# The first token tile leads the projection at a layer's beginning

## The chip, the cores and the metric

The kernel runs on one core of one Trainium2 chip. The metric is the time of one execution on the device in microseconds (us), the median of several runs. The engines are named as in the profile: PE is TensorE (products), PEld its weight loads, DVE VectorE, ACT ScalarE, POOL GpSimd, SP the queue that issues DMAs.

## The reference

Two layers of a decoder, in float32, for 256 tokens of 2048 features. Each layer is a norm, a mixer with an input and an output projection, a second norm and a residual:

```python
def rms_norm(x, g):
    xf = x.astype(jnp.float32)
    y = xf * lax.rsqrt(jnp.mean(xf * xf, axis=-1, keepdims=True) + RMS_EPS)
    return (y * g.astype(jnp.float32)).astype(x.dtype)
...
for layer in range(DEPTH):            # 2
    g_pre, g_post, p = layer_params[layer]
    h = rms_norm(x, g_pre)
    h = even_mixer(h, *p) if layer % 2 == 0 else odd_mixer(h, *p)
    x = x + rms_norm(h, g_post)
...
# even_mixer (RG-LRU and mLSTM):  u = h @ w_in (2048 x 8192); ...; y @ w_out (4096 x 2048)
# odd_mixer (RWKV-7):             u = h @ w_in (2048 x 16384); loras of h; ...; y @ w_out (4096 x 2048)
```

## The kernel before

**Tokens and features.** The 256 tokens are two token tiles of 128, counted by `tt`. Norms have tokens on the partitions; `x` lies in four tiles `xs[c]` of [128, 2 token tiles, 512 features]. The input projections have features on the partitions, so the normed tokens are turned by products: `to_features` multiplies a 128x128 block of `xs` with `dg[tt]`, a diagonal matrix of the token tile's 1/rms (`scale`, made from `rstd`), and so turns and scales in one. Each such f32 product shows as two records in the trace (`mb<-dg,xq` and `gb<-dg,xq` in layer 0, `xr` in layer 1).

**Two parts.** Projections run in fp32r. For precision each operand is split into a high part and the rest: `hh`, `hl` for the tokens (ACT copies with the norm's weight as scale, DVE subtracts), `whi`, `wlo` for the weights (`split_w`, the same two engines). Each product of a block is then three: hh with whi, hl with whi, hh with wlo.

**The input projection.** `in_proj` makes 512 output features at a time, in two PSUM banks `gb`; its depth of 2048 is cut into 8 pieces of two k-tiles. A piece is one DMA of 512 KB (`raw`, 4 buffers), one split (`whi`, `wlo`, 3 buffers each), and 24 products (`in_mms`: 8 blocks x 3) of 128x128 weights with 256 columns, both token tiles at once. Piece `pc` reads k-tiles 2 pc and 2 pc + 1 of `h`, that is half of one of the four tiles `hh[c]`, `hl[c]`. Layer 0 has 16 such projections of 512 features, layer 1 has 32 and the loras.

**The output projection.** `out_proj` has tokens on the partitions, four chunks of 512 features. In the last chunk the last pieces (`NLAST` = 3 and up to `ROOM` = 3 more) go token tile by token tile, so that `evac` (sum of squares, `rstd`, product with the post-norm's weight) and `after` (residual `xs`, its squares, the next norm's `scale`) of tile 0 run beside the products of tile 1. What `evac` and `after` emit for tile 1 comes behind the last product.

**The beginning of a layer.** In layer 0: load `x` tile by tile, keep-warm products (`W0` = 14, bf16, read by nothing), squares of both tiles on ACT, both `scale`, then `to_features`. In layer 1: `to_features` directly behind `out_proj` of layer 0, with `W1` = 6 and `W2` = 10 keep-warm products before and between the first transposes. `to_features` turns tile 0 of c = 0, 1 and 2, then for each c turns tile 1 (for c = 3 both) and splits 256 columns at a time into `hh` and `hl`: 16 ACT and 16 DVE operations a layer. Then `in_proj` begins:

```python
banks = [gbank(), gbank()]
for pc in range(8):
    in_mms(banks, *split_w(load_w(wsrc[pc])), pc, h, 4, 0.44)
return banks
```

**Order.** PE issues in the order of the program (`InOrder`). ACT, DVE, POOL and SP are ordered when the program is built, by priorities: weight splits are raised by `AHEAD` = 1000 and the last tile's `evac` and `after` by 2000, and with `Behind` what is emitted after a weight split on ACT or DVE stays behind it. Steps of the mixers are woven between the products of a projection by amounts of product work (`tick`). All engines work in order once built.

**Lines.** The helpers record their operations under one line: products are L116, transposes by identity L119, ACT and DVE operations L132, DMAs of weight pieces L217; the two POOL steps of `rstd` are L312 (scale by 1/D and add EPS) and L314 (power -0.5), the residual's store is L720.

## Time and profile before

| | |
|---|---|
| three runs | 1916.69, 1919.91, 1921.01 us (median 1919.91) |
| profiled execution | span 1912.7 us from its first to its last instruction; the profile gives no other time of it |
| busy | PE 98%, weight loads 91%, DVE 73%, ACT 55%, POOL 3% |
| mean granted clock | 0.997 |
| products | 16498 records, each with a weight load |

The runs are times of whole executions, the span is that of one other, profiled execution of the same kernel; the median is 7.2 us above it. In the timeline a row has start, length, engine, line, operation, `out<-in`, shapes, count and, in brackets, the engine's idle time before it and what ended that. In the groups, `| busy us, mean ns of one | idle before`. The granted clock (PEclk) is 1.00 at full speed.

### The profile page before, as it was taken

The page shows a single profiled execution, that of the slowest core. Times are in us where ns is not written, and L with a number is a line of the kernel's source. Part 1 is how long each engine was busy: PE and PEld are TensorE (multiplying, and loading weights), DVE is VectorE, ACT ScalarE, POOL GpSimd, SP SyncE. Part 2 cuts the span into 40 slices and gives each one's busy share as a digit, 9 for nine tenths or more (in the row PEclk, how much of TensorE's full clock was granted, in tenths as well). Part 3 has the DMA queues.
Part 4 walks back from the last instruction along what each step waited for, and adds up shares of the span by engine and source line. Part 5 has one row for each costly group of instructions (what it writes and reads, how often), then busy time and mean ns, then how long its engine had stood idle before and what let it go on. Part 6 is the DMA issues. An engine that isn't in the chain of part 4 may idle for free.

```text
span 1912.7 us, 39517 instructions
## 1 busy us (share of the span) xinstructions
PE 1883.4 (98%) x16498; PEld 1747.9 (91%) x16498; DVE 1395.3 (73%) x2302; ACT 1044.1 (55%) x1609; POOL 60.4 (3%) x84
## 2 busy tenths in 40 slices
PE   8999999999999999999999999999999999999998
PEld 7999999999888899989999999999999999997886
DVE  5667777757554569969689689597796896895544
ACT  5444666645444546555565555655655655555442
POOL 0000000000000100000000000000000000000000
PEclk9999999999999999999999999999999999999999
DMA  7433545455666444434444434344344443356664
GB/s 250 142 133 111 177 162 169 155 171 194 215 208 195 168 147 135 152 118 144 133 136 138 133 130 155 111 147 149 113 150 139 136 136 131 122 187 203 211 202 156
DMA packets 86947, 299.63 MB, mean 157 GB/s; under 512 B 9576, under 2 KB 12392, under 8 KB 86768
## 3 DMA queue, kind: packets, MB, share of 16 engines
q1 hardware_dynamic: 86768, 297.11, 47.2%
q8 instruction: 129, 2.11, 0.5%
q14 instruction: 50, 0.41, 0.1%
HBM read 289.20 MB, written 7.86 MB: 155 GB/s over the span
## 4 chain that ended last, share of the span: by engine, by line
PE 93%; DVE 4%; ACT 1%; issue 1%; DMA 0%; POOL 0%; SPq 0%; DVEq 0%; POOLq 0%; ACTq 0%
PE gb L116 75%; PE mb L116 17%; DVE wlo L132 2%; PE mb L119 1%; DVE wb L132 1%; ACT whi L132 1%; DMA xq<-in_x_dram 0%; DVE rt L132 0%; DVE Tb L132 0%; DVE tf L132 0%; DVE Ab L132 0%; DVE yT L132 0%; ACT ZT L132 0%; ACT vt L132 0%; DVE At L132 0%
## 5 line engine op out<-in xcount | busy, mean ns | idle before, releaser
L132 DVE TENSOR_TENSOR wlo<-raw,whi 128x1024 fp32r<-128x1024 f32 x509 | 619.9, 1219 | 338.0 <-ACT whi L132 304.5
L132 ACT CAST whi<-raw 128x1024 fp32r<-128x1024 f32 x509 | 532.6, 1048 | 557.3 <-PE gb L116 512.3
L116 PE MATMUL gb<-hh,whi 128*128 128x256 f32 x3120 | 790.5, 289 | 2.8 <-ACT whi L132 2.8
L116 PE MATMUL gb<-hl,whi 128*128 128x256 f32 x3120 | 770.6, 283 | 0.0
L116 PEld LDWEIGHTS gb<-hh,whi 128*128 128x128 f32 x3120 | 596.7, 191 | 13.6 <-ACT whi L132 3.7
L116 PEld LDWEIGHTS gb<-hl,whi 128*128 128x128 f32 x3120 | 597.5, 192 | 0.8
L116 PE MATMUL gb<-hh,wlo 128*128 128x256 f32 x3120 | 453.5, 286 | 0.0
L116 PEld LDWEIGHTS gb<-hh,wlo 128*128 128x128 f32 x3120 | 404.9, 191 | 4.2 <-issue 0.7
L116 PE MATMUL gb<-whi,yl 128*128 128x512 f32 x500 | 136.9, 392 | 0.5 <-DVE yl L132 0.5
L116 PE MATMUL gb<-whi,yh 128*128 128x512 f32 x500 | 136.5, 392 | 0.0
L116 PE MATMUL gb<-wlo,yh 128*128 128x512 f32 x500 | 135.7, 390 | 0.0
L116 PEld LDWEIGHTS gb<-whi,yl 128*128 128x128 f32 x500 | 93.2, 188 | 20.4 <-DVE yl L132 0.9
L116 PEld LDWEIGHTS gb<-wlo,yh 128*128 128x128 f32 x500 | 93.5, 188 | 19.8
L116 PEld LDWEIGHTS gb<-whi,yh 128*128 128x128 f32 x500 | 93.0, 188 | 19.3
L132 DVE TENSOR_TENSOR Tb<-Tb,tf 64x31 f32<-64x31 f32 (+15 forms) x248 | 82.6, 333 | 6.1
L132 DVE TENSOR_TENSOR tf<-Ab,Tb 64x31 f32<-64x31 f32 (+15 forms) x248 | 81.9, 330 | 4.5
L116 PE MATMUL mb<-AR,BK 64*128 64x128 f32 (+1 forms) x1024 | 58.0, 253 | 7.0 <-DVE AR L132 6.0
L116 PEld LDWEIGHTS mb<-AR,BK 64*128 64x128 f32 (+1 forms) x1024 | 50.2, 161 | 13.3 <-PE gb L116 7.1
L132 DVE TENSOR_TENSOR UV<-mb,Gn 64x256 f32<-64x256 f32 x64 | 26.9, 421 | 34.5 <-PE mb L116 33.4
L132 ACT ACTIVATE zz<-kP,dv 128x256 f32<-128x256 f32 x64 | 32.3, 505 | 22.9 <-DVE kP L132 12.4
L116 PEld LDWEIGHTS mb<-UV,At 128*64 128x64 f32 (+1 forms) x1024 | 35.0, 137 | 10.3 <-issue 2.5
L1125 POOL TENSOR_TENSOR vr<-vr,mhalf 128x8 f32<-128x8 f32 x16 | 28.3, 1771 | 499.4 <-DVE vr L132 499.4
(258 smaller groups left out, 1855.9 us busy)
## 6 DMA issues: line engine op xcount, KB each, us to landing
raw<-in_w_in_dram SPq DMA_DIRECT2D x384, 512.0 KB, 3.3
raw<-in_w_out_dram SPq DMA_DIRECT2D x128, 512.0 KB, 4.3
y1d<-zt SPq DMA_DIRECT2D x7, 512.0 KB, 3.9
yraw<-y1d SPq DMA_DIRECT2D x7, 512.0 KB, 4.3
l<-in_lora_dram SPq DMA_DIRECT2D x8, 384.0 KB, 4.6
xq<-in_x_dram SPq DMA_DIRECT2D x8, 256.0 KB, 5.2
lw<-in_lruw_dram SPq DMA_DIRECT2D x4, 512.0 KB, 4.6
xr<-in_x_dram SPq DMA_DIRECT2D x8, 256.0 KB, 6.0
```

Of the source, the lines that this page charges most:

```text
L116: return self._chain(self.eng.matmul(*a, **k))
L119: return self._chain(self.eng.transpose(**k))
L132: r = op(*a, **k)
L1125: pool.tensor_tensor(vr, vr, mhalf[:, 0:8], ALU.pow)
```

## The change

1. `to_features` works by token tile. `turn(tt)` makes all 16 transposes of one tile, one `mb` bank for each c, and returns four splits; each is 4 ACT and 4 DVE operations of 128 columns. It returns `h` and the turn of tile 0, and leaves the turn of tile 1 in the list `rest`. Its keep-warm products (`W1`, `W2`) are gone; `W0` is 20.
2. The first `in_proj` of a layer finds `rest` filled. It loads and splits `LEAD` = 3 pieces, makes their 72 products with the 128 columns of tile 0, then the transposes and splits of tile 1, then the same 72 products with tile 1; pieces 3 to 7 go as before.
3. In layer 0 tile 0 is scaled, turned and split before the squares of tile 1 are emitted. In layer 1 `out_proj` gets `between`: behind the last products of tile 1 come the transposes of the next layer's tile 0; the first of their splits goes between `evac` and `after`, the others behind `after`.
4. `rstd` loses its POOL step L312: the squares are scaled by D ** -0.5 on ACT (`RD`), and EPS is a fifth column of the sums, set once by a POOL memset.

Comments are dropped as well. The diff without these, cut to its core:

```diff
-W0, W1, W2 = 14, 6, 10
+W0 = 20
+LEAD = 3
...
-    def in_mms(banks, hi, lo, pc, h, nft, tick):
+    def in_mms(banks, hi, lo, pc, h, nft, tick, tts=None):
+        to = 0 if tts is None else tts * P
+        tn = T if tts is None else P
         def mm(part, kk, f, hx, first=False, last=False):
-            pe.matmul(banks[f // 2][:, (f % 2) * T:(f % 2 + 1) * T], lhsT=part[:, kk, f * P:(f + 1) * P], rhs=hx,
-                      start=first, stop=last, skip_group_check=True)
+            pe.matmul(banks[f // 2][:, (f % 2) * T + to:(f % 2) * T + to + tn], lhsT=part[:, kk, f * P:(f + 1) * P],
+                      rhs=hx[:, to:to + tn], start=first, stop=last, skip_group_check=True)
...
+    rest = []
     def in_proj(wsrc, h):
         banks = [gbank(), gbank()]
-        for pc in range(8):
+        lead = LEAD if rest else 0
+        ws = [split_w(load_w(wsrc[pc])) for pc in range(lead)]
+        for tt in range(2):
+            for pc in range(lead):
+                in_mms(banks, *ws[pc], pc, h, 4, 0.22, tt)
+            if rest:
+                for split in rest.pop()():
+                    split()
+        for pc in range(lead, 8):
             in_mms(banks, *split_w(load_w(wsrc[pc])), pc, h, 4, 0.44)
...
     # out_proj, last pieces of the last chunk, for each tt
+                parts = between() if tt and between else []
                 with tc.high_priority(offset=2 * AHEAD):
                     evac(c, banks, (tt,))
+                    for split in parts[0:1]:
+                        split()
                     after(tt)
+                for split in parts[1:]:
+                    split()
...
     def rstd(ss):
         dve.tensor_reduce(ms, ss, mybir.AxisListType.X, ADD)
-        pool.tensor_scalar(ms, ms, 1.0 / D, EPS, MUL, ADD)
         pool.tensor_tensor(rs, ms, mhalf[:, 0:1], ALU.pow)
     def sums(n):
-        return [sp.tile([P, 4], F32, name=f"{n}{tt}", tag=f"{n}{tt}") for tt in range(2)]
+        ts = [sp.tile([P, 5], F32, name=f"{n}{tt}", tag=f"{n}{tt}") for tt in range(2)]
+        for t in ts:
+            pool.memset(t[:, 4:5], EPS)
+        return ts
...
-    def to_features(xs, dg, g, warm):
+    def to_features(xs, dg, g):
-        h = []
-        banks[2] = [gbank(), gbank()]
-        keep_warm(warm[0], banks[2][0])
-        for c in range(2):
-            turn(c, 0)
-        keep_warm(warm[1], banks[2][0])
-        turn(2, 0)
-        for c in range(4):
-            if c == 3:
-                turn(c, 0)
-            turn(c, 1)
-            ... (hh, hl of 256 columns, i = 0 to 3)
+        h = [tuple(hp.tile([P, 4, T], F32R, name=n, tag="hp") for n in ("hh", "hl")) for c in range(4)]
+        def turn(tt):
+            ts, parts = slice(tt * P, (tt + 1) * P), []
+            def split(c, b):
+                hh, hl = h[c]
+                for f in range(4):
+                    bf = b[:, f * P:(f + 1) * P]
+                    activ(hh[:, f, ts], bf, AF.Copy, scale=g(4 * c + f))
+                    dve.scalar_tensor_tensor(hl[:, f, ts], bf, g(4 * c + f), hh[:, f, ts].bitcast(F32), MUL, SUB)
+            for c in range(4):
+                b = mbank()
+                for f in range(4):
+                    pe.matmul(b[:, f * P:(f + 1) * P], lhsT=xs[c][:, tt, f * P:(f + 1) * P], rhs=dg[tt],
+                              start=(f == 0), stop=True, skip_group_check=True)
+                parts.append(lambda c=c, b=b: split(c, b))
+            return parts
+        rest.extend([lambda: [], lambda: turn(1)])
+        return h, lambda: turn(0)
...
     # layer 0
         for tt in range(2):
             for c in range(4):
-                activ(sq[c][:, tt, :], xs[c][:, tt, :], AF.Square, acc=ss[tt][:, c:c + 1])
-        h = to_features(xs, [scale(ss[tt], s0) for tt in range(2)], lambda i: vs0("pre", i), (0, 0))
+                activ(sq[c][:, tt, :], xs[c][:, tt, :], AF.Square, scale=RD, acc=ss[tt][:, c:c + 1])
+            dg.append(scale(ss[tt], s0))
+            if tt == 0:
+                for split in first():
+                    split()
```

## The prediction

> **What bounds the kernel now.** I read the page first: the busy shares (part 1) and the chain that ended last (part 4).

> ```profile
> span 1912.7 us, 39517 instructions
> ...
> PE 1883.4 (98%) x16498; PEld 1747.9 (91%) x16498; DVE 1395.3 (73%) x2302; ACT 1044.1 (55%) x1609; POOL 60.4 (3%) x84
> ...
> PE 93%; DVE 4%; ACT 1%; issue 1%; DMA 0%; POOL 0%; SPq 0%; DVEq 0%; POOLq 0%; ACTq 0%
> ```

> TensorE is busy in 98% of the span and carries 93% of the chain. A product added to TensorE therefore costs its full cadence, unless it falls into one of the few holes. The change works in two holes, at the beginning of each layer, so I read next the timeline of TensorE there. Columns: start, length, engine, line, what it does, count, and in brackets the idle time before it. First layer 0, with the cast and the rest of the first weight piece from ScalarE and VectorE:

> ```profile
> 9.64 2.05 PE L116 MATMUL mb<-dg,xq 128*128 128x128 f32 x16 [3.60 <-DVE dg L132]
> 11.53 1.06 PE L116 MATMUL gb<-dg,xq 128*128 128x128 f32 x8
> 12.72 1.05 ACT L132 CAST whi<-raw 128x1024 fp32r<-128x1024 f32 x1 [0.94 <-DMA raw<-in_w_in_dram]
> 13.26 2.05 PE L116 MATMUL mb<-dg,xq 128*128 128x128 f32 x16 [0.68 <-DVE dg L132]
> 13.80 1.23 DVE L132 TENSOR_TENSOR wlo<-raw,whi 128x1024 fp32r<-128x1024 f32 x1 [0.59 <-ACT whi L132]
> 15.15 1.06 PE L116 MATMUL gb<-dg,xq 128*128 128x128 f32 x8
> 16.81 2.02 PE L116 MATMUL mb<-dg,xq 128*128 128x128 f32 x16 [0.60 <-PE gb L116]
> 18.59 0.36 PE L116 MATMUL gb<-hh,whi 128*128 128x256 f32 x1
> ...
> 27.29 0.28 PE L116 MATMUL gb<-hh,whi 128*128 128x256 f32 x1
> ```

> From 9.64 to 18.59 there are 64 transpose records (two per f32 product, 32 per token tile) and less than 2 us of idle time; at 18.59 the projection begins, and at 27.29 its fourth piece. Then layer 1, the same view, with what VectorE does ahead of the first piece's low part:

> ```profile
> 642.71 0.61 PE L116 MATMUL gb<-wlo,yh 128*128 128x512 f32 x2
> 643.17 1.47 PE L116 MATMUL gb<-ones 128*128 128x512 bf16 x6
> 644.22 0.68 DVE L132 TENSOR_TENSOR og<-gb,gp 128x512 f32<-128x512 f32 x1
> 644.48 1.95 PE L116 MATMUL mb<-dg,xr 128*128 128x128 f32 x16
> 645.25 2.74 DVE L132 SCALAR_TENSOR_TENSOR xr<-og,rs,xr 128x512 f32<-128x512 f32 x4 [0.35 <-POOL rs L314]
> 646.26 2.32 PE L116 MATMUL gb<-ones 128*128 128x512 bf16 x10
> 647.91 1.22 DVE L132 TENSOR_TENSOR wlo<-raw,whi 128x1024 fp32r<-128x1024 f32 x1
> 648.42 1.05 PE L116 MATMUL gb<-dg,xr 128*128 128x128 f32 x8
> 651.38 2.47 PE L116 MATMUL mb<-dg,xr 128*128 128x128 f32 x16 [1.91 <-DVE dg L132]
> 653.64 1.92 PE L116 MATMUL gb<-dg,xr 128*128 128x128 f32 x8
> 655.35 2.39 PE L116 MATMUL mb<-dg,xr 128*128 128x128 f32 x16
> 657.50 0.36 PE L116 MATMUL gb<-hh,whi 128*128 128x256 f32 x1
> ...
> 666.21 0.28 PE L116 MATMUL gb<-hh,whi 128*128 128x256 f32 x1
> ```

> Here the hole is real: 14.3 us from 643.17 to 657.50, of which 7.5 are transposes that stay and the rest is keep-warm products, 1.91 us of idle time, and transposes drawn out by the granted clock. The table of windows (PE, PEld, DVE, ACT and POOL busy, then PEclk) has it at 0.58 there:

> ```profile
> 652.90:656.90 4.00, 4.00 (x23) 4.00 (x23) 3.88 (x10) 3.27 (x9) 0.00 (x0) 0.58 0.58 209
> ```

> **The price that decides: a projection product of 128 columns.** Three pieces are 72 products of 256 columns; the change makes them 144 of 128 columns in each layer, and each still loads its own 128x128 weights. No row has such a product in fp32r, so I bound it. The groups and runs below give mean lengths of weight loads (PEld) and lengths of runs of products; a run's cadence is (length - one) / (count - 1).

> ```profile
> L116 PEld LDWEIGHTS gb<-hl,whi 128*128 128x128 f32 x3120 | 597.5, 192 | 0.8
> L116 PEld LDWEIGHTS mb<-cs,sq 128*128 128x128 f32 x128 | 15.2, 192 | 1.1 <-ACT sq L132 1.1
> L116 PEld LDWEIGHTS mb<-ZT,Aab 32*32 32x32 f32 x512 | 16.8, 108 | 1.3 <-issue 0.4
> L116 PEld LDWEIGHTS <-ones 128*128 128x128 bf16 x30 | 3.1, 110 | 5.6 <-issue 2.1 <-DVE ones L132 1.4
> ...
> 26.33 1.12 PE L116 MATMUL gb<-hh,wlo 128*128 128x256 f32 x8
> 68.19 1.95 PE L116 MATMUL mb<-we,xm 128*128 128x128 f32 x16
> 726.79 1.84 PE L116 MATMUL mb<-cs,sq 128*128 128x2 f32 x16
> 810.86 2.21 PE L116 MATMUL mb<-ZT,Aab 32*32 32x32 f32 x64
> ```

> The 256-column projection product: (1.12 - 0.28)/7 = 0.120 us. The product of cs and sq moves only 2 columns and still runs at (1.84 - 0.25)/15 = 0.106: what it waits for can only be the load of its 128x128 weights. Where the weights are 32 columns wide, the cadence falls to (2.21 - 0.19)/63 = 0.032. The projection's load takes 192 ns like that of cs and sq. So I take it that halving the columns leaves the cadence at the weight load. The bounds are 0.106 from below and 0.120 from above; between them lies the f32 product of the same 128x128 form, (1.95 - 0.28)/15 = 0.112, which I take as the nearest. One token tile of three pieces then costs 72 x 0.112 = 8.1 us, nearly as much as both together cost now (72 x 0.120 = 8.6).

> [...]

> **The change, part by part.** Transposes run at (2.05 - 0.28)/15 = 0.118 a record, 32 x 0.118 = 3.8 us a tile.

> Layer 0. The first tile's transposes can start at about 9.4 (its norm loses one POOL operation) and end at 13.2, but the first product waits for the cast of the first piece, 12.72 + 1.05 = 13.8, a DMA's landing that the change leaves alone; that hides the norm's gain and the six added keep-warm products (W0), which run before 9.4. Then: 13.8 + 8.1 (tile 0) + 3.8 (turn of tile 1, its scale long there, since dg came at 13.2) + 8.1 (tile 1) = 33.8 for the beginning of the fourth piece, against 27.29: **+6.5 us**.

> Layer 1. The transposes of tile 0 take the place of the keep-warm products at 643.17 and end at 647.0. The 16 products with the first piece's high part end at 648.8. Its low part came at 647.91 + 1.22 = 649.1; now four quarter splits go ahead of the residual on VectorE, about 0.3 us each, partly in its 0.35 idle, so I take 650.0: a new wait of 1.2. The other 56 products take 6.3 (656.3), the turn 3.8 (660.1), tile 1 8.1: 668.2, against 666.21: **+2.0 us**. The second norm is hidden: needed at 656.3, late by a microsecond at most against 651.38.

> The end. Each norm loses a POOL step, which counts only where nothing covers it, in the last tile's:

> ```profile
> 1906.12 0.19 POOL L312 TENSOR_SCALAR ms<-ms 128x1 f32<-128x1 f32 x1 [3.31 <-DVE ms L132]
> 1906.40 0.56 POOL L314 TENSOR_TENSOR rs<-ms,mhalf 128x1 f32<-128x1 f32 x1
> ```

> From start to start 0.28: **-0.3 us**. The memsets of EPS go to POOL, busy 3%, early; the scale in the squares is free.

> The splits. 16 halves become 32 quarters on each of two engines:

> ```profile
> L132 ACT ACTIVATE hh<-mb,vec 128x256 fp32r<-128x256 f32 x12 | 5.3, 488 | 0.2 <-PE mb L116 0.2
> L132 DVE SCALAR_TENSOR_TENSOR hl<-mb,vec,hh 128x256 fp32r<-128x256 f32 x12 | 5.2, 477 | 0.2 <-ACT hh L132 0.2
> L132 ACT CAST bones<-cs 128x128 fp32r<-128x128 f32 x1 | 0.3, 296 | 0.0
> ```

> At about 0.30 each (the 128x128 cast), 32 x 0.30 = 9.6 against 16 x 0.48 = 7.7: about 2 us more on each engine, beside 16 us of products, nothing on the path. If the cover goes, the third piece waits for the second bank's splits, or the turn of tile 1 for its four PSUM banks, which VectorE must have emptied; in layer 0 the worst is three casts (3 x 1.05) ahead of the splits, +3.2, in layer 1 I allow 1.5. The three weight pairs are all held until tile 1 reads them, so the fourth piece's cast waits for the first 16 products of tile 1; two pieces (48 x 0.112 = 5.4 us) cover its 1.05 + 1.23. On SP the three piece loads keep their places relative to each other; the next load comes no earlier and is needed 6 us later in layer 0. The keep-warm products of layer 1 go; with TensorE busy and one wait of 1.2 I take no clock loss. Before, 40 transposes took 6.1 us from 651.38 for 40 x 0.118 = 4.7, so a drop costs up to 1.4.

> Sum: 6.5 + 2.0 - 0.3 = **+8.2 us**, a span of 1920.9. The median of the three runs is 7.2 us above the profiled span; leaving that as it is, 1919.9 + 8.2 = **1928.1 us**.

> Bounds: a cadence of 0.106 takes off 288 x 0.006 = 1.7, no wait for the low part 1.2: +5.3. A cadence of 0.120 adds 2.3, the splits late in layer 1 1.5, the clock 1.4: +13.4. So 1925 to 1933 for this case.

> **The rivals.** First, the other side: the fp32r weight load can be hidden as well as the stream, and a product of half the columns costs half, 0.060. Layer 0: 13.8 + 4.3 + 3.8 + 4.3 = 26.2 (-1.1). Layer 1: high part until 648.0, the low part at 650.0, 56 x 0.060 = 3.4, 3.8, 4.3: 661.5 (-4.7). With the end -6.1: 1913.8. The sum in the cadence p is 272 p - 22.4 (144 products in layer 0, 128 in layer 1 behind its wait), so the sign turns at 0.082. For it: the stream alone explains 0.120 at 256 columns as well as the load does. Against it: the 2-column product at 0.106.

> Second, half of the load is hidden: 0.086, midway between 0.060 and 0.112. A tile costs 6.2; layer 0 30.0 (+2.7), layer 1 650.0 + 4.8 + 3.8 + 6.2 = 664.8 (-1.4), end -0.3: +1.0, 1920.9, no change. [...]

> Third, the tile doesn't lead: the order on ScalarE and VectorE puts its splits behind the second norm. Layer 0 would begin after four quarter splits behind the first hl (14.9 + 1.3 = 16.2, +2.4 more), layer 1 after dg at about 651.9 and the splits: 653 + 8.1 + 3.8 + 8.1 = 673 (+6.8). Sum 6.5 + 2.4 + 6.8 - 0.3 = +15.4: 1935.3. For it: casts of weights stand ahead of splits in the rows of layer 0; against it: the new code raises the first bank's splits ahead of the residual.

> Fourth, a short fp32r product runs like two records of f32, 0.224: 288 x 0.112 = 32.3 more, 1960. No row speaks for it but that f32 itself does so.

> **How the numbers follow.** My case 0.62, the first rival 0.14, the second 0.11, the third 0.09, the fourth 0.04. About 0.2%, 3.8 us, is what a measurement can tell from no change. Slower: 0.62 + 0.09 + 0.04 = 0.75; faster 0.14; same 0.11. The range takes in my case, the second and the third rival (0.82): 1918.5 to 1935.5.

> **What would show it.** Right: runs of 128-column products in gb at 0.106 to 0.120; weight loads still 192 ns; the fourth piece about 6 us later in layer 0 and about 2 us in layer 1; 7 more us of products in gb per layer. A cadence near 0.06 makes the forecast wrong in sign; long waits of TensorE for hl or for banks would show the third rival.

## The result, and the profile after

| | before | changed |
|---|---|---|
| median of the runs | 1918.54 us (4 runs, 1916.69 to 1921.01) | 1937.08 us (4 runs, 1935.48 to 1938.25) |
| ratio | | 1.0097, 95% interval 1.0085 to 1.0109 |
| profiled span | 1912.7 us | 1933.7 us |
| mean granted clock | 0.997 in the profiled run, 0.992 to 0.996 in the timed ones | 0.989 to 0.991 |

The change costs 18.5 us, about twice the forecast of 8.2, and the time lies above the range of 1918.5 to 1935.5. The page of the changed kernel:

```profile
span 1933.7 us, 39849 instructions
...
PE 1907.6 (99%) x16632; PEld 1772.8 (92%) x16632; DVE 1400.5 (72%) x2334; ACT 1050.3 (54%) x1641; POOL 59.1 (3%) x84
```

TensorE is busy in 99% of the span, 24 us longer than before. Not all of that is added work: a product that runs at a lower clock counts as busy for longer (eight products 1.91 us at half clock and 1.06 at full, in the rows below). The timeline of TensorE at the beginning of layer 0, to be laid beside the one of before (the fourth piece began at 27.29 there; L118 is the products' line now):

```profile
9.13 3.84 PE L118 MATMUL mb<-dg,xq 128*128 128x128 f32 x32 [1.06 <-DVE dg L134]
14.79 0.33 PE L118 MATMUL gb<-hh,whi 128*128 128x128 f32 x1 [1.83 <-ACT whi L134]
...
17.17 1.91 PE L118 MATMUL gb<-hh,wlo 128*128 128x128 f32 x8
...
29.12 5.69 PE L118 MATMUL mb<-dg,xq 128*128 128x128 f32 x32
34.56 0.30 PE L118 MATMUL gb<-hh,whi 128*128 128x128 f32 x1
...
36.38 1.06 PE L118 MATMUL gb<-hh,wlo 128*128 128x128 f32 x8
...
42.63 0.34 PE L118 MATMUL gb<-hh,whi 128*128 128x256 f32 x1
```

The same eight products take 1.91 us at 17.17 and 1.06 at 36.38: a cadence of (1.91 - 0.41)/7 = 0.214 and of (1.06 - 0.28)/7 = 0.111. The table of windows shows what differs (PE, PEld, DVE, ACT, POOL busy, then PEclk, DMA share, GB/s):

```profile
12.60:16.00 3.40, 1.57 (x15) 1.38 (x13) 2.42 (x7) 2.93 (x7) 0.22 (x1) 1.00 0.94 351
16.00:19.40 3.40, 3.40 (x19) 3.40 (x17) 3.40 (x7) 2.19 (x5) 0.00 (x0) 0.50 0.76 263
...
29.60:33.00 3.40, 3.40 (x18) 3.40 (x17) 0.70 (x2) 0.86 (x3) 0.00 (x0) 0.50 0.00 0
33.00:36.50 3.50, 3.50 (x34) 3.50 (x32) 2.59 (x10) 2.90 (x11) 0.00 (x0) 0.99 0.00 0
```

At 16.0, behind a stretch with 1.57 us of product time in 3.40, the granted clock falls to half and stays there for 17.1 us, although TensorE is busy all the time (the rows from 19.4 to 29.6, left out here, have 0.50 as well). Layer 1, where the fourth piece came 23.04 us after the output projection (643.17 to 666.21):

```profile
658.58 3.73 PE L118 MATMUL mb<-dg,xr 128*128 128x128 f32 x32
662.07 0.31 PE L118 MATMUL gb<-hh,whi 128*128 128x128 f32 x1
...
665.15 1.11 PE L118 MATMUL gb<-hh,wlo 128*128 128x128 f32 x8 [1.06 <-DVE wlo L134]
...
671.46 3.79 PE L118 MATMUL mb<-dg,xr 128*128 128x128 f32 x32
675.00 0.31 PE L118 MATMUL gb<-hh,whi 128*128 128x128 f32 x1
...
683.07 0.33 PE L118 MATMUL gb<-hh,whi 128*128 128x256 f32 x1
```

Here the clock held in the profiled run: 24.49 us, 1.45 more than before. The groups of this stretch (busy us, mean ns of one) have the weight loads as long as ever:

```profile
L118 PEld LDWEIGHTS gb<-hh,whi 128*128 128x128 f32 x53 | 10.2, 192 | 0.0
```

The timeline of the end shows the norm without its POOL step, 0.24 us from reduction to power where it was 0.52 (1905.88 to 1906.40 before):

```profile
1927.12 0.16 DVE L134 TENSOR_REDUCE ms<-sq 128x1 f32<-128x5 f32 x1 [0.57 <-ACT gp L134]
1927.36 0.56 POOL L335 TENSOR_TENSOR rs<-ms,mhalf 128x1 f32<-128x1 f32 x1 [3.58 <-DVE ms L134]
```

**Where the 21.0 us of the two profiled runs went.** Fourth piece of layer 0: +15.3. Between there and layer 1: nothing. Layer 1: +1.5. After that the instructions on TensorE are the same in the same order, and their distance to those of before grows in three steps of 1.4 to 1.6 us, each at a stretch with the clock at half that before did not have; a fourth, at 1610, has its twin before at 1588. The first of the three:

```profile
845.50:848.90 3.40, 3.40 (x27) 3.05 (x27) 2.55 (x7) 0.51 (x1) 0.00 (x0) 0.50 0.20 78
```

That is 15.3 + 1.5 + 4.4 - 0.2 = 21.0. The runs of before lay between 1916.2 and 1922.5, at mean clocks between 0.992 and 0.996, where its profiled run had 0.997: that run was one with few short falls. Each kernel has one profile, so of the other runs only the mean clock is known, and not where it fell. A run is best read by its span times its mean clock, which is nearly the same in all runs of one kernel (e1: within 2.7 us, where its spans lie 11.1 apart):

| kernel | median us | mean clock of its runs | span x clock, us |
|---|---|---|---|
| before (23 runs) | 1919.47 | 0.992 to 0.996 | 1904.7 to 1908.3 |
| changed | 1937.08 | 0.989 to 0.991 | 1915.2 to 1916.4 |
| e1, layer 0's hole filled | 1932.07 | 0.990 to 0.996 | 1915.7 to 1918.4 |
| e8, both holes filled | 1927.04 | 0.995 to 0.996 | 1916.1 to 1917.6 |
| e7, before with its hole filled | 1916.34 | 0.994 to 0.998 | 1904.9 to 1908.2 |

The change adds about 10 us at full clock, waits included, and some 8 us by the clock. The 10 fit the places above: 15.3 less half of the 17.1 us at half clock, 1.5 in layer 1 and the 1.7 that before had lost there in its own fall (653 to 656), less 0.2 at the end.

### The profile page after: what moved, and what is told of

The parts are those of the page before. It is cut to its first block, busy times and chain, and to the rows that moved or that the text cites. A ratio compares the mean times of both kernels' runs of the same rounds, so it can differ in the third digit from the quotient of the medians.

```text
span 1933.7 us, 39849 instructions
## 1 busy us (share of the span) xinstructions
PE 1907.6 (99%) x16632; PEld 1772.8 (92%) x16632; DVE 1400.5 (72%) x2334; ACT 1050.3 (54%) x1641; POOL 59.1 (3%) x84
## 4 chain that ended last, share of the span: by engine, by line
PE 94%; DVE 4%; ACT 1%; issue 1%; DMA 0%; POOL 0%; SPq 0%; DVEq 0%; POOLq 0%; ACTq 0%
PE gb L118 76%; PE mb L118 17%; PE mb L121 1%; DVE wlo L134 1%; ACT whi L134 0%; DMA xq<-in_x_dram 0%; DVE rt L134 0%; DVE Tb L134 0%; DVE wb L134 0%; DVE tf L134 0%; DVE Ab L134 0%; DVE yT L134 0%; ACT ZT L134 0%; ACT vt L134 0%; DVE xr L134 0%
## 5 line engine op out<-in xcount | busy, mean ns | idle before, releaser
L118 PE MATMUL gb<-hh,whi 128*128 128x256 f32 (+1 forms) x3168 | 806.4, 290 | 4.7 <-ACT whi L134 4.7
L118 PE MATMUL gb<-hl,whi 128*128 128x256 f32 (+1 forms) x3168 | 786.6, 284 | 0.0
L118 PEld LDWEIGHTS gb<-hh,whi 128*128 128x128 f32 x3168 | 609.4, 192 | 15.7 <-ACT whi L134 5.7
L118 PEld LDWEIGHTS gb<-hl,whi 128*128 128x128 f32 x3168 | 610.5, 193 | 0.8
L118 PE MATMUL gb<-hh,wlo 128*128 128x256 f32 (+1 forms) x3168 | 462.1, 287 | 1.1 <-DVE wlo L134 1.1
L118 PEld LDWEIGHTS gb<-hh,wlo 128*128 128x128 f32 x3168 | 412.9, 192 | 5.4 <-DVE wlo L134 1.2
L118 PE MATMUL gb<-whi,yl 128*128 128x512 f32 x500 | 136.9, 392 | 0.5 <-DVE yl L134 0.5
L118 PE MATMUL gb<-whi,yh 128*128 128x512 f32 x500 | 136.5, 392 | 0.0
L118 PE MATMUL gb<-wlo,yh 128*128 128x512 f32 x500 | 135.7, 390 | 0.0
L118 PEld LDWEIGHTS gb<-whi,yl 128*128 128x128 f32 x500 | 93.2, 188 | 20.3 <-DVE yl L134 0.9
L118 PEld LDWEIGHTS gb<-wlo,yh 128*128 128x128 f32 x500 | 93.5, 188 | 19.8
L118 PEld LDWEIGHTS gb<-whi,yh 128*128 128x128 f32 x500 | 93.0, 188 | 19.3
L118 PE MATMUL mb<-AR,BK 64*128 64x128 f32 (+1 forms) x1024 | 57.9, 253 | 6.9 <-DVE AR L134 5.9
L118 PEld LDWEIGHTS mb<-AR,BK 64*128 64x128 f32 (+1 forms) x1024 | 50.1, 161 | 13.3 <-PE gb L118 7.0
L134 DVE TENSOR_TENSOR UV<-mb,Gn 64x256 f32<-64x256 f32 x64 | 26.9, 420 | 34.3 <-PE mb L118 33.1
L134 ACT ACTIVATE zz<-kP,dv 128x256 f32<-128x256 f32 x64 | 32.3, 505 | 22.8 <-DVE kP L134 12.4
L118 PEld LDWEIGHTS mb<-UV,At 128*64 128x64 f32 (+1 forms) x1024 | 35.0, 137 | 10.3 <-issue 2.2
L118 PE MATMUL mb<-UV,At 128*64 128x64 f32 (+1 forms) x1024 | 43.8, 228 | 0.0
```

Source lines behind the costliest of these rows:

```text
L118: return self._chain(self.eng.matmul(*a, **k))
L134: r = op(*a, **k)
```

## The experiments

My theory after the result was that two things add up: the 128-column products run at the cadence of their weight loads, as forecast, and the clock falls in layer 0's hole and isn't given back while such products run. The rival for the cadence of 0.214 was contention: the DMAs' share is near 1 at the beginning of layer 0 (0.94, 0.76 and 1.00 in the windows from 12.6 to 22.8), and ACT and DVE split at the same time.

**e1: fill the hole of layer 0.**

```diff
             if tt == 0:
-                for split in first():
+                parts0 = first()
+                keep_warm(8, gbank())
+                for split in parts0:
                     split()
```

> The changed kernel with 8 keep-warm products between the transposes of tile 0 and the first projection product of layer 0 (a hole of 1.83 us there). Clock theory: the hole lets the granted clock fall to half at 16.0 us, and the load-bound 128-column products cannot bring it back until 33.1 us. Then here the clock stays at 1.00, the products run at 0.112 us instead of 0.213, the fourth piece begins at 14.8 + 8.1 + 3.8 + 8.1 = 34.8 us instead of 42.6, and the time is 1937.1 - 7.8 = about 1929. Rival, contention (DMAs at a share of 1.0 and both splitting engines slow the weight loads in that stretch): the cadence stays at 0.213 and the time at 1937.

Measured: 1932.07 us (1925.69 to 1936.75), 1.0068 of before (1.0046 to 1.0091). Layer 0 is as the clock theory has it, under a DMA share that is no lower (0.90, where the row at half clock had 0.76; the table of windows of e1):

```profile
16.00:22.80 6.80, 6.80 (x64) 6.80 (x62) 6.68 (x24) 4.20 (x12) 0.00 (x0) 1.00 0.90 339
```

The timeline of e1 has the fourth piece:

```profile
34.38 0.34 PE L118 MATMUL gb<-hh,whi 128*128 128x256 f32 x1
```

It begins 8.25 us earlier than in the changed kernel, so contention is out as the cause of the 0.214. But the median gave back only 5.0, and the runs lie 11 us apart. In the profiled run the clock fell in layer 1 instead, at 659.1, for 10.2 us, behind the 1.05 us wait for `wlo`, and the fourth piece there came 29.4 us after the output projection (650.27 to 679.65); the windows of e1:

```profile
655.70:659.10 3.40, 2.35 (x21) 2.26 (x21) 2.96 (x6) 2.38 (x7) 1.40 (x1) 1.00 0.66 235
659.10:665.90 6.80, 6.80 (x34) 6.80 (x34) 5.46 (x22) 2.82 (x10) 0.00 (x0) 0.50 0.52 174
665.90:669.30 3.40, 3.40 (x18) 3.40 (x18) 0.01 (x1) 0.37 (x1) 0.00 (x0) 0.50 0.00 0
669.30:676.00 6.70, 6.70 (x62) 6.70 (x61) 4.88 (x16) 5.41 (x16) 1.07 (x2) 1.00 0.00 0
```

The changed kernel has the same instructions there and the same wait, and its profiled run kept the clock. The traces show one difference. In a trace the clock's changes lie on a grid. In the trace of before and in that of the changed kernel each lies a whole number of 3.4133 us from every other: the short falls take 3.413, the long one of the changed kernel 17.067 (5 times), and from its fall at 16.0 to that at 845.5 it is 829.44 (243 times). The place of the grid differs: counted from the span's start, its first point is at 0.90 us in the trace of before, at 2.36 in that of the changed kernel, and at about 0.3 in e1, by its fall at 659.1. In e1 the whole wait lies in one such window, with 2.35 us of products (the first row above). In the changed kernel's trace the grid, carried on from its falls at 16.0 and 845.5, cuts the wait in two; its windows:

```profile
661.14:664.55 3.41, 2.95 (x27) 2.81 (x25) 3.41 (x8) 3.41 (x11) 0.00 (x0) 1.00 0.61 231
664.55:667.97 3.42, 2.82 (x25) 2.82 (x26) 2.98 (x6) 1.84 (x6) 1.40 (x1) 1.00 0.69 238
```

By these two traces it was luck that the clock held in layer 1 there.

**e2: lead in layer 1 only.** An in-projection with a norm before it takes its lead from a list, one entry a layer:

```diff
+    LEADS = [0, 3]
...
-        lead = LEAD if rest else 0
+        lead = LEADS.pop(0) if rest else 0
```

> The lead of three pieces in layer 1 only; in layer 0 both tiles are turned before the first piece (LEAD = 0 there), all else as changed. If the loss lies in layer 0: no half clock there, the first product at about 17 us (dg of tile 1 at 13.2, 32 records x 0.118), the fourth piece at about 25.8 instead of 27.3 before; layer 1 as in the changed kernel (+1.5 us against before); the time 1918.5 - 1.5 + 1.5 - 0.3 = about 1918, give or take 1.5 us for each fall of the clock later in layer 1. If the 128-column products are the loss wherever they stand: about 1928.

Measured: 1932.6 us (1928.33 to 1935.32), a miss of 14.6 us, and by neither of the two reasons named. Layer 0's first product came at 23.31, not at 17 (the timeline of e2):

```profile
16.86 6.70 PE L118 MATMUL mb<-dg,xq 128*128 128x128 f32 x32 [3.80 <-DVE hl L134]
23.31 0.36 PE L118 MATMUL gb<-hh,whi 128*128 128x256 f32 x1
```

The turn of tile 1 waits 3.80 us for VectorE's splits of tile 0: the four `mb` banks are full. And in that wait the clock fell, from 15.4 for 6.8 us. So the changed kernel's order needs the lead as cover for its own splits. In layer 1 the clock fell as in e1 (10.2 us).

**e3: lead with one piece in both layers** (the same edit).

```diff
+    LEADS = [1, 1]
```

> LEAD = 1 in both layers. Clock theory (what brings the clock back is a window of products that stream all the time, which the f32 transposes do and load-bound 128-column products do not): the clock falls at 16.0 as with three pieces, the transposes of tile 1 begin at about 18.8 instead of 29.1, and the clock is back by 22.8 to 26.2 instead of 33.1: two or three windows of 3.4 us instead of five. Fourth piece of layer 0 at about 32.7. Rival (the half clock lasts a fixed 17 us): back at 33.1. Weight-load theory for layer 1: two pieces less at 24 x (2 x 0.112 - 0.120) = 2.5 us each, less 1.3 of new waiting for dg: 3.5 us less than changed, so about 2 us less than before. Time 1937.1 - 10 - 3.5 = about 1924.

Measured: 1925.85 us (1923.12 to 1929.3). In layer 0 the clock fell at 16.7 and was back at 20.1, behind one window, not two or three, and not 17 us. The timeline of e3, and then its windows:

```profile
17.50 4.25 PE L118 MATMUL mb<-dg,xq 128*128 128x128 f32 x24
```

```profile
16.70:20.10 3.40, 3.40 (x18) 3.40 (x18) 2.76 (x9) 2.98 (x8) 0.00 (x0) 0.50 0.96 379
20.10:23.50 3.40, 2.91 (x25) 2.69 (x24) 3.40 (x11) 2.59 (x9) 0.00 (x0) 1.00 0.92 324
```

The transposes began at 17.50 and filled most of that window; a fixed length is out. That streaming is what brings the clock back was my theory; the run shows only that it came back behind transposes. The fourth piece came at 31.68 (32.7 expected). In layer 1 the clock fell again for 10.2 us, which the expectation had not counted: that the time came within 2 us of the 1924 expected is in part luck.

**e5: 64 columns.** e1 with each leading product of tile 0 in two halves, 144 instead of 72 a layer.

```diff
+            step = 64 if tts == 0 else tn
+            for o in range(to, to + tn, step):
+                pe.matmul(banks[f // 2][:, (f % 2) * T + o:(f % 2) * T + o + step], lhsT=part[:, kk, f * P:(f + 1) * P],
+                          rhs=hx[:, o:o + step], start=first and o == to, stop=last, skip_group_check=True)
```

> e1_fill with each leading product of tile 0 made as two of 64 columns (144 instead of 72 a layer), all else as there. Weight-load theory: the cadence stays at 0.106 to 0.112 us although the columns halve, so 72 x 0.11 = 8 us more in each layer, 16 in all against e1_fill. Rival (the cadence follows the columns streamed plus a fixed cost): 0.112 would fall towards 0.08 or less, and the added time would be below 8 in all.

Measured: 1969.01 us in the one run, 37 us above e1's median and more than either side said. The timeline of e5 (x2 is two products):

```profile
15.15 0.39 PE L118 MATMUL gb<-hh,whi 128*128 128x64 f32 x2
15.38 0.39 PE L118 MATMUL gb<-hl,whi 128*128 128x64 f32 x2
...
21.45 0.61 PE L118 MATMUL gb<-hh,whi 128*128 128x64 f32 x2
21.88 0.61 PE L118 MATMUL gb<-hl,whi 128*128 128x64 f32 x2
```

Its windows:

```profile
15.20:18.60 3.40, 3.40 (x33) 3.40 (x32) 3.40 (x6) 2.88 (x6) 0.00 (x0) 0.99 0.75 248
18.60:25.40 6.80, 6.80 (x34) 6.80 (x33) 6.17 (x32) 2.13 (x7) 0.00 (x0) 0.50 0.89 357
...
42.50:45.90 3.40, 3.40 (x18) 3.40 (x18) 0.70 (x2) 0.90 (x3) 0.00 (x0) 0.51 0.02 5
45.90:49.30 3.40, 3.40 (x33) 3.40 (x32) 2.58 (x10) 2.84 (x11) 0.00 (x0) 1.00 0.00 0
```

From 15.15 to 18.28 there are 14 such rows, so two products take 0.224 us at full clock, 0.11 each as with 128 columns: the cadence is the weight load's. At half clock it is (21.88 - 21.45)/2 = 0.215, so the load runs with the clock (in the changed kernel's trace a load takes 192 ns in the mean from 36.4 to 42 us, at full clock, and 333 from 19 to 29, at half). And the clock fell at 18.6 in a stretch in which TensorE did not wait once, and came back at 45.9, behind the first window full of transposes (from 41.93). In layer 1 it fell in the same way, at 680.7 for 23.9 us, where e1's profiled run had 10.2. Half of 27.3 is 13.7, half of the 13.7 more in layer 1 is 6.8; with the 16 us of doubled loads that is 36.5, against 37.2 between the two profiled spans.

**e8: hold the clock in both layers.** e1, with 5 keep-warm products between the high and the low part of the first leading piece of layer 1 (in `in_mms`; none in layer 0).

```diff
+        if tts == 0 and pc == 0 and WLO.pop(0):
+            keep_warm(WLO[0], gbank())
...
+    WLO = [0, 1, 5]
```

> The changed kernel with the clock held in both layers: 8 keep-warm products in the hole of layer 0 and 5 in the wait for the first low part in layer 1 (1.06 us). Expected by the clock theory: no half clock in either layer's beginning in the profile, fourth piece 7.1 us later than before in layer 0, and 23.3 + 1.5 = 24.7 us from the last product of the output projection to the fourth piece of layer 1; the time 1919.2 + 7.1 + 1.5 - 0.3 = about 1927.5, which is the sum of the prediction, and the runs closer together than those of e1_fill (1925.7 to 1936.8). If the 128-column products let the clock fall by themselves: layer 1 at 29 us again and about 1932.

Measured: 1927.04 us (1925.60 to 1928.56), 1.0039 of before (1.0026 to 1.0053), and the runs 3 us apart. No half clock in either beginning; a window of e8, and the fourth piece of layer 1 in its timeline:

```profile
657.50:663.00 5.50, 5.50 (x52) 5.50 (x51) 5.06 (x16) 3.07 (x12) 1.17 (x1) 1.00 0.82 262
```

```profile
674.78 0.33 PE L118 MATMUL gb<-hh,whi 128*128 128x256 f32 x1
```

Fourth piece of layer 0 at 34.36, +7.1; layer 1 from 650.29 to 674.78, 24.49, +1.45. The mean clock of all five runs lies at 0.995 to 0.996, so the profiled one is no exception.

**e10: e8 with one leading piece.**

```diff
+    LEADS = [1, 1]
...
-        lead = LEAD if rest else 0
+        lead = LEADS.pop(0) if rest else 0
```

> e8_fill_both with a lead of one piece instead of three. With the clock held, a leading piece costs 24 x (2 x 0.1115 - 0.120) = 2.5 us: the fourth piece of layer 0 at 34.4 - 5.0 = 29.4 us (27.3 before); in layer 1 the two pieces saved come with about 1.3 us of new waiting for the second norm, so 24.7 - 3.7 = 21.0 us (23.3 before). The time about 1919.2 + 2.1 - 2.3 - 0.3 = 1919, no change. If the loss were in the order of the splits and not in the products, layer 0 would stay at 34.

Measured: 1926.17 us (1923.68 to 1926.52), a miss: 0.9 less than with three pieces where 8 were expected. The fourth piece of layer 0 came at 32.06, not 29.4. The turn of tile 1 waits for banks in both layers (the timeline of e10):

```profile
20.98 1.16 PE L118 MATMUL mb<-dg,xq 128*128 128x128 f32 x8 [1.46 <-DVE hl L134]
...
660.70 5.29 PE L118 MATMUL mb<-dg,xr 128*128 128x128 f32 x24 [2.85 <-DVE hl L134]
```

In layer 1 the clock fell in these waits (6.8 us from 658.8). A shorter lead saves weight loads and uncovers the splits.

**e9: turn tile 0 early, but lead with nothing.** Two of tile 1's transposed banks are `gb`, the splits of both tiles alternate, and 19 keep-warm products stand in layer 1's hole.

```diff
+        def second():
+            b1 = [turn(1, c, gbank()) for c in range(2)]
+            split(1, 0, b1[0])
+            for c in range(1, 4):
+                split(0, c, b0[c])
+                if c < 3:
+                    b1.append(turn(1, c + 1, mbank()))
+                split(1, c, b1[c])
```

> Tile 0 is turned early as in the change, but no piece leads: every projection product has 256 columns. The turn of tile 1 takes two of its four banks from the projection's, the splits of both tiles alternate, and 19 keep-warm products stand in the wait for the second norm in layer 1. If the lead's doubled weight loads are the loss and the early turn is worth its transposes: layer 0 begins its products at about 17.0 us (18.6 before), layer 1 12.2 us after the output projection (14.6 before), the end 0.3 less: 1919.2 - 1.6 - 2.3 - 0.3 = about 1915. If the splits of 128 columns can't keep up, the products begin as late as before or later: 1919 or more.

Measured: 1923.3 us (1919.96 to 1925.96), 1.0019 of before (1.0010 to 1.0027). The second outcome: the splits can't keep up (the timeline of e9).

```profile
16.80 2.05 PE L118 MATMUL mb<-dg,xq 128*128 128x128 f32 x16 [1.85 <-DVE hl L134]
...
658.21 2.08 PE L118 MATMUL mb<-dg,xr 128*128 128x128 f32 x8 [3.33 <-DVE hl L134]
```

Layer 0 begins its products at 18.60 as before (18.59); layer 1 loses 3.33 us to the bank, and in that wait the clock fell for 6.8 us (from 657.5).

**e7: the kernel before, with its own hole filled** (`W2` 18 instead of 10) and the shorter norm; no lead. The diff is against the kernel before:

```diff
-W0, W1, W2 = 14, 6, 10
+W0, W1, W2 = 14, 6, 18
+RD = D ** -0.5
...
-        pool.tensor_scalar(ms, ms, 1.0 / D, EPS, MUL, ADD)
...
-                activ(sq[c][:, tt, :], xs[c][:, tt, :], AF.Square, acc=ss[tt][:, c:c + 1])
+                activ(sq[c][:, tt, :], xs[c][:, tt, :], AF.Square, scale=RD, acc=ss[tt][:, c:c + 1])
```

> The kernel before, with two small edits: 8 more keep-warm products in the hole of layer 1 (W2 18 instead of 10; TensorE sat idle there for 1.91 us and the clock fell to half for 3.4 us behind it), and the changed kernel's shorter norm (no POOL step). No token tile leads. Expected by the clock theory: no fall of the clock at the beginning of layer 1, so 40 transposes at 0.118 instead of 6.1 us (-1.4), dg of tile 1 0.3 to 1 us earlier, the end 0.3 earlier: about 2 to 3 us less than before, 1916 to 1917. If keep-warm products don't hold the clock, 0.5 us less at most.

Measured: 1916.34 us (11 runs), 0.9984 of before (0.9975 to 0.9993), the lowest median of all. The clock holds in layer 1's beginning; the timeline of e7, and a window:

```profile
646.43 4.05 PE L117 MATMUL gb<-ones 128*128 128x512 bf16 x18
...
655.10 2.02 PE L117 MATMUL mb<-dg,xr 128*128 128x128 f32 x16 [1.05 <-DVE hl L133]
```

```profile
650.00:653.00 3.00, 3.00 (x28) 2.87 (x26) 2.53 (x11) 1.15 (x3) 0.68 (x1) 1.00 0.92 270
```

The gain in the place itself is smaller than expected (first product 13.8 us after the start of the output projection's last product instead of 14.6): transposes at full clock now wait 1.05 for the splits. So the places explain about 1 us of the 3.1: 0.8 there, and the 0.24 of the shorter norm at the end. The rest lies in the clock: span times clock is that of before, and the runs' mean clock is higher. Which falls went away is not shown; the profiled run had one in layer 0, from 9.1 for 3.4 us, that the profiled run of before did not have. No run separates the two edits, and that 1916.3 met the expected 1916 to 1917 is in part luck.

## Why the prediction was wrong, point by point

- **The direction was right, and so was the price of a product at full clock.** Cadence of the 128-column product: 0.112 forecast, 0.111 measured at full clock; 64 columns run at the same 0.11 (e5), so it is the weight load, and the fp32r load is 192 ns as in the rows of before. The first, second and fourth rival (cheaper or dearer products) fall by that.
- **The sum, where the clock holds, was right in its parts.** They are, in e8: layer 0 +7.1 (6.5 forecast), layer 1 +1.45 (2.0), the new wait for the first low part 1.06 in the changed kernel (1.2), the end -0.24 (-0.3). That makes 8.3, against 8.2. That e8's median lies 7.6 above before is a weaker match than it looks: at full clock the two are about 10 apart, and e8 kept a higher mean clock than before.
- **The step that failed is the clock's**: "with TensorE busy and one wait of 1.2 I take no clock loss", and the bound beside it, "a drop costs up to 1.4". Layer 0 was forecast to have its fourth piece at 33.8 and had it at 42.63. Of these 8.8 us, 6.2 are tile 0's products (14.79 to 29.12, 14.3 us for 8.1) and 1.6 the turn of tile 1 (5.4 for 3.8), both mostly at half clock; the other 1.0 is in the next point. In layer 1 the same can happen and costs 4.9 (29.4 instead of 24.5, e1). The bound came from the only row of the kind before, one window of 3.4 us over transposes. It left out that a fall can last longer than that window (17.1 us here), and that a load's cadence follows the clock. Here the fall lasted until the transposes of tile 1 came, and the cadence of the products before them went from 0.111 to 0.214.
- **The hole of layer 0 was too small.** I had the transposes end at 13.2 and the first product at 13.8. It came at 14.79: ACT puts the cast of the first piece behind the squares of tile 1 and the first splits, at 13.71 instead of 12.72. The 1.0 us costs itself, and the fall came behind the hole of 1.83 us; with the hole filled, it does not occur in the profiled runs (e1, e8).
- **The third rival** (the tile doesn't lead) did not happen, though the time lies 1.8 us from its 1935.3: tile 0's products began at 14.79 and, in layer 1, directly behind its transposes. Its reason, late splits, is what a shorter lead meets (e2, e9, e10): there the turn of tile 1 waits for its PSUM banks, by up to 3.80 us. That danger the prediction had, with at most 3.2 us in layer 0 and 1.5 in layer 1. With three pieces the lead covers it.
- **The median against the profile.** I carried the 7.2 us between the profiled span and the median over unchanged. Of them 1.8 are the difference between a run's time and its span, the same in every run (1935.48 and 1933.7 for the changed kernel's profiled one). The rest goes with the clock: 0.997 in the profiled run, 0.992 to 0.996 in the others. The changed kernel's profile has more short falls than that of before (four of 3.4 us against two, without the one that each has at its end); that the change itself moved their number is not shown.
- Why a lead can hardly win here, by a sum and not by a run of its own: a leading piece in the hole fills 24 x 0.111 = 2.7 us of it, and its second half costs 2.7 again, where the whole piece costs 24 x 0.120 = 2.9. At best it gives back 0.2 us a piece. e7 fills layer 1's hole without a lead.

## What to carry to other kernels

Before cutting a product's columns, compare its cadence with that of a product with hardly any columns and the same weights: here they were alike, 0.120 us with 256 columns and 0.106 with 2, and two halves cost 2 x 0.111 = 0.222, nearly twice the whole. Price a hole in TensorE's work not by its length alone but by what runs behind it: in these runs 128-column products did not bring the clock back, and ran at half speed until the transposes came (0.214 us each instead of 0.111, from 16.0 to 29.1 in the changed kernel, behind a hole of 1.83). When runs of one kernel scatter, multiply each span by its mean clock before explaining the scatter by the code.

## What the runs showed of the hardware

```profile
7.72:11.13 3.41, 1.49 (x13) 1.49 (x14) 0.45 (x2) 2.56 (x9) 0.75 (x2) 1.00 1.01 351
```

- Among the windows with 128-column products and the wait for `wlo`, 2.35 us of product time (e1) and 2.69 (e2, the row below) were followed by a fall, 2.82 and 2.95 (changed) were not. This was not measured further, nor whether the product time alone decides.

```profile
653.74:657.15 3.41, 2.69 (x24) 2.69 (x25) 2.97 (x6) 1.96 (x6) 1.40 (x1) 1.00 0.67 231
```

- 128-column products held a full clock (e8, 657.5 to 663.0) but did not restore it in three whole windows and most of a fourth (changed, 16.0 to 29.1); 64-column ones lost it (e5); f32 transposes restored it by the end of the first or second window that they ran in (33.1 changed, 669.3 e1, 20.1 e3, 45.9 e5). That the time in which columns stream is what counts, and not the time in which weights load, is my explanation; no run measures it.
- The cadence of the load-bound products nearly doubles at half clock, 0.111 to 0.214 us with 128 columns (changed) and 0.112 to 0.215 with 64 (e5).
- The fall in layer 1 comes in some runs only, with the same instructions in the same order. The two traces above have it depend on where the window lies against the hole; no run varied this alone.
